# Two hybrid encoder layers on one core: score products over all 128 rows with stacked operands, units of q and k one step ahead, a gate back in the attention

## The chip, the cores and the metric

The kernel runs on 1 core of a Trainium2 chip. The metric is device time in microseconds: the median of the runs, beside one profiled execution, from whose trace all single durations are taken.

## The reference

Two layers over a sequence x of 512 tokens and 1024 channels. In each layer one input projection of x feeds three branches, whose outputs are gated, added and projected; then comes a layer norm. The change is in branch B, the differential attention:

```python
def _diff_attention(q, k, v, lam):           # 8 heads, 2 halves c of 64 channels each
    ...
    def block(qblk):
        s = jnp.einsum('bqhcd,bkhcd->bhcqk', qblk, k) * scale
        p = jax.nn.softmax(s.astype(jnp.float32), axis=-1)
        w = p[:, :, 0] - lam * p[:, :, 1]
        return jnp.einsum('bhqk,bkhe->bqhe', w, vf)
...
merged = (gates[:, :, 0] * (y_ssd @ w_br_ssd) + gates[:, :, 1] * (y_diff @ w_br_diff)
          + gates[:, :, 2] * (y_cross @ w_br_cross))      # gates = sigmoid(x @ w + b)
```

q and k go through a rotary embedding first. Branch A is a state-space scan (SSD) in both directions with 32 heads, branch C a cross attention into 256 memory tokens.

## The kernel before

Every large product is made in three passes: each operand is split into a high part (a copy by ACT, rounded to the matmul's format) and a low part (DVE: the value less its high part), and low times high, high times low and high times high add up in one bank of PSUM (`mm3`, line 103 for the matmul itself). Weights come in **units** of 128 x 1024 values: SP loads one (wr), ACT and DVE split it (wh, wl), and `proj` runs 24 products of 128 x 512 over it. `self.T` collects the whole program as a plan of units and steps; `emit` loads a unit two plan places ahead, into two buffers wr, and splits it into three buffers wh and wl.

The order on PE in the attention is written out by hand (`manual_schedule`). On DVE, ACT and SP the scheduler of the framework sets the order from its own costs when the kernel is built, and the engine then takes its instructions one after another in that order. Each DMA is issued by SP, which also stands still in its queue until what the next DMA waits for is there.

A layer runs its branches A, C and B one after the other and then the output projection. In branch A, four groups g of four blocks b: `zpart` is a unit, `ypart` builds for two heads the masked decay matrices (ab: a DMA, DVE, eight times ACT's exp, DVE) into m, and PE multiplies m with xsT (pm<-m,xsT). As PE has less work there than the others, gates of branches C and B that are needed later are computed in between: the table AHEAD names after which (g, b) which gate (branch, block) stands. A gate computed ahead is stored to memory (dgt<-tg) and loaded again in its branch.

In branch B, a head h has one unit each for q, k, v and the gate path g (two halves of a unit pair make the v of two heads). `rope` takes a unit's product out of PSUM (ACT, into rx), lets four DMAs write it with its 32-row quarters swapped (rsw), and adds rx times cos and rsw times sin on DVE. The result x has the first half c = 0 of the head's channels in rows 0 to 63 and the second in rows 64 to 127, and is split into q0 and q1, or k0 and k1 (high and low). `scores` works on a block of 128 queries (s = 4h + block): per half c three products over 64 rows, into a bank each; DVE takes the row minimum of each bank (fmx; q carries a factor of -1/8), ACT the exponential, and DVE the difference of the two maps (fpp). `turn` transposes fpp on PE and splits it (wT), `values` multiplies with v.

The attention is a list of steps s = 0 to 34, and each carries one unit: first the scores of s + 1, then half of the unit, then `values` and `turn` of s, then the other half. What a unit gives is needed by a later step, and its work on ACT, DVE and SP runs beside PE. For head h the units stand as rope(h + 1, q), rope(h + 1, k) and then two of g (h even) or two of v (h odd).

```python
units += [rope(h + 1, "q"), rope(h + 1, "k")]
units += [gpart(h), gpart(h + 1)] if h % 2 == 0 else [vpart(h + 1), vpart(h + 2)]
```

Seven of the eight gates of B follow as the last units (`gate(j)`); the eighth, block 0, is in AHEAD.

## Time and profile before

| | |
|---|---|
| median of 3 runs | 2222.38 us (2219.97 to 2222.85) |
| profiled execution, its own time | 2223.68 us |
| its span | 2221.9 us, granted clock of TensorE 0.997 |
| busy share of the span | PE 98%, DVE 71%, ACT 45%, POOL 2% |
| first attention, 715 to 985 us | PE busy 268.34 of 270 us |
| score products (pm<-k,q) | 384 of 64 x 128 by 64 x 512 |
| transfers | 283.73 MB, queue of SP 42.4% of 16 engines' span |

PE is TensorE's matmuls, PEld its weight loads, DVE VectorE, ACT ScalarE, POOL GpSimd, and SPq the queue in which SyncE issues DMAs. A row of the timeline has the start and the length in us, then engine, line, operation and the tiles; matmuls overlap in the records, so their spacing is read from start to start. A row of the waits has the time in all, how often, and the longest.

### The profile page before, as it was taken

Reading aid. Unit: us, or ns where it says so; the run is one execution under the profiler, and the core shown is the slowest. Engines: PE = TensorE matmul, PEld = TensorE weight load, DVE = VectorE, ACT = ScalarE, POOL = GpSimd, SP = SyncE. Lnnn points to the kernel's source line nnn. Section 1 sums busy time; section 2 is a strip of 40 time slices with the busy share of each in tenths; the row PEclk is TensorE's granted clock in tenths of the full one; section 3 lists DMA queues with packets and bytes.
Section 4 is the critical chain, followed back from the end, with each engine's and each line's share of the span. In section 5 each row is a group of like instructions: output and inputs, shape, how many; then the busy total and the mean of one; then the engine's idle time right before and its main releaser. Section 6 shows DMA issues by size and latency. Waiting matters only on the chain.

```text
span 2221.9 us, 29523 instructions
## 1 busy us (share of the span) xinstructions
PE 2171.0 (98%) x11330; PEld 1768.0 (80%) x11330; DVE 1585.9 (71%) x2440; ACT 1004.3 (45%) x1895; POOL 54.2 (2%) x38
## 2 busy tenths in 40 slices
PE   8999999999999999999999999999999999999998
PEld 6787877788887888878887777777788887888786
DVE  7887878758554777766467888888754547777567
ACT  5664545424442454543355564545423324554440
POOL 0000000000000000000000100000100000000000
PEclk9999999999999999999999999999999999999999
DMA  4654554425553322224564654454434333222353
GB/s 149 182 160 144 144 136 144 125 86 167 168 173 117 95 85 79 77 89 147 152 214 122 177 146 145 133 152 132 124 105 132 105 113 94 75 84 81 91 154 112
DMA packets 106162, 283.73 MB, mean 128 GB/s; under 512 B 12524, under 2 KB 13092, under 8 KB 105764
## 3 DMA queue, kind: packets, MB, share of 16 engines
q1 hardware_dynamic: 106020, 281.84, 42.4%
q8 instruction: 89, 1.46, 0.3%
q14 instruction: 53, 0.43, 0.1%
HBM read 255.55 MB, written 17.85 MB: 123 GB/s over the span
## 4 chain that ended last, share of the span: by engine, by line
PE 71%; DVE 14%; DMA 8%; ACT 5%; issue 1%; POOL 0%; SPq 0%; POOLq 0%; DVEq 0%; ACTq 0%
PE pj L103 55%; PE pm L103 13%; DMA ab<-dab 5%; DVE wl L81 3%; PE pt L111 2%; DVE ab L81 2%; DVE acc L84 2%; ACT ab L91 1%; ACT wh L91 1%; DMA wr<-wu 1%; DVE y L81 1%; DVE rx L81 1%; PE pt L103 1%; DMA fth<-rd 1%; DVE m L81 1%
## 5 line engine op out<-in xcount | busy, mean ns | idle before, releaser
L103 PE MATMUL pj<-xh,wl 128*128 128x512 f32 x1664 | 669.2, 402 | 11.0 <-DVE wl L81 8.9
L103 PE MATMUL pj<-xh,wh 128*128 128x512 f32 x1664 | 661.0, 397 | 0.0
L103 PE MATMUL pj<-xl,wh 128*128 128x512 f32 x1664 | 658.5, 396 | 0.0
L81 DVE TENSOR_TENSOR wl<-wr,wh 128x1024 fp32r<-128x1024 f32 x330 | 405.7, 1230 | 109.0 <-ACT wh L91 108.1
L91 ACT ACTIVATE wh<-wr 128x1024 fp32r<-128x1024 f32 x330 | 347.4, 1053 | 228.4 <-PE pj L103 147.4
L103 PEld LDWEIGHTS pj<-xh,wl 128*128 128x128 f32 x1664 | 313.9, 189 | 91.2 <-issue 18.3
L103 PEld LDWEIGHTS pj<-xh,wh 128*128 128x128 f32 x1664 | 313.8, 189 | 71.7 <-issue 5.7
L103 PEld LDWEIGHTS pj<-xl,wh 128*128 128x128 f32 x1664 | 314.2, 189 | 63.6 <-issue 3.6
L91 ACT ACTIVATE ab<-ab,bias 128x128 f32<-128x128 f32 x512 | 160.8, 391 | 120.5 <-DVE ab L81 119.7
L84 DVE SCALAR_TENSOR_TENSOR acc<-pj,hcw,acc 128x510 f32<-128x510 f32 x192 | 142.4, 744 | 24.2 <-ACT acc L91 22.8
L91 ACT ACTIVATE fpp<-pm,fmx 128x512 f32<-128x512 f32 x128 | 87.9, 687 | 84.3 <-DVE fmx L889 83.6
L889 DVE TENSOR_REDUCE fmx<-pm 128x1 f32<-128x512 f32 x128 | 87.0, 686 | 45.9 <-PE pm L103 45.5
L103 PE MATMUL pj<-yl,wh 128*128 128x512 f32 x256 | 102.4, 400 | 0.9 <-DVE yl L84 0.9
L103 PE MATMUL pj<-yh,wh 128*128 128x512 f32 x256 | 103.0, 403 | 0.0
L81 DVE TENSOR_TENSOR ab<-ab,cst 128x1024 f32<-128x1024 f32 x64 | 85.4, 1334 | 24.4 <-DMA ab<-dab 24.4
L103 PE MATMUL pj<-dy,wh 128*128 128x512 f32 (+1 forms) x384 | 102.2, 354 | 0.1
L103 PE MATMUL pj<-yh,wl 128*128 128x512 f32 x256 | 102.0, 399 | 0.0
L103 PE MATMUL pj<-cy,wh 128*128 128x512 f32 x256 | 78.8, 389 | 0.0
L103 PEld LDWEIGHTS pj<-dy,wh 128*128 128x128 f32 x384 | 67.8, 189 | 11.0 <-DVE dy L81 0.9
L103 PE MATMUL pj<-wh,xl 128*128 128x256 f32 x256 | 74.8, 292 | 0.0
L81 POOL TENSOR_TENSOR sqa<-sqa,sz 128x512 f32<-128x512 f32 x32 | 52.9, 1654 | 845.6 <-ACT sz L91 845.6
L103 PE MATMUL pj<-wl,xh 128*128 128x256 f32 x256 | 72.4, 283 | 0.0
(273 smaller groups left out, 3269.1 us busy)
## 6 DMA issues: line engine op xcount, KB each, us to landing
wr<-wu SPq DMA_DIRECT2D x336, 512.0 KB, 3.7
ab<-dab SPq DMA_DIRECT2D x64, 512.0 KB, 5.7
eb<-deb SPq DMA_DIRECT2D x64, 256.0 KB, 4.7
mkv<-dkv SPq DMA_DIRECT2D x16, 512.0 KB, 4.5
rsw<-rx SPq DMA_DIRECT2D x128, 64.0 KB, 2.0
dgt<-tg SPq DMA_DIRECT2D x18, 256.0 KB, 2.8
dkv<-mo SPq DMA_DIRECT2D x16, 256.0 KB, 4.2
dkv<-q SPq DMA_DIRECT2D x16, 256.0 KB, 3.6
```

Source lines behind the costliest of these rows:

```text
L81: (eng or self.nc.vector).tensor_tensor(out=out, in0=a, in1=b, op=op)
L84: self.nc.vector.scalar_tensor_tensor(out=out, in0=a, scalar=s, in1=b, op0=op0, op1=op1)
L91: self.nc.scalar.activation(out=out, in_=a, func=f, **kw)
L103: self.nc.tensor.matmul(out=out, lhsT=a, rhs=b, start=first, stop=last)
L111: self.nc.tensor.transpose(out=out, in_=x, identity=self.ident)
L889: nc.vector.tensor_reduce(out=mx[:, c:c + 1], in_=ps, axis=AX.X, op=ALU.min)
```

## The change

- **Stacked operands.** `rope` splits into one tile qkh with two planes, high and low, and four more DMAs stack them by half c. For k: k0 and k1 are now one tile for each half c, with the high part in rows 0 to 63 and the low part in rows 64 to 127. For q: a tile for each half and head, with both planes twice, in rows 0 to 63 and again in rows 64 to 127; it lies in the place that dy0 takes later (the tile of all q is called dy0).
- **Scores.** Per half c two products over 128 rows, ql and then qh against the stacked k, half 0 first, then half 1. (Low times low is added too.)
- **Order of units.** q of head 1 stands before the attention's steps. For head h come rope(h + 1, k), the two of g or v, then rope(h + 2, q): k a step earlier than before, q a whole head ahead of its use.
- **Gates.** Block 0 of B's gate is again a unit of the attention, without its way through memory. In the SSD's last group the one other gate stands behind b = 1 instead of b = 0.
- **Tiles.** dy is made only after the last scores; the residual of the output projection is loaded into fth, the next layer's memory rows into qkh.

```diff
-         (2, 0): [(2, 5)], (2, 2): [(2, 6)], (3, 0): [(2, 7)], (3, 2): [(1, 0)]}
+         (2, 0): [(2, 5)], (2, 2): [(2, 6)], (3, 1): [(2, 7)]}
...
-                self.qk[h, nm] = [self.t(fp, [P, S], f"{nm}{i}", F32R) for i in range(2)]
-                self.split(*self.qk[h, nm], x)
+                hl = self.t(fp, [P, 2, S], "qkh", F32R)
+                self.split(hl[:, 0, :], hl[:, 1, :], x)
+                half = [slice(64 * c, 64 * c + 64) for c in range(2)]
+                if nm == "q":
+                    o = [self.qst[:, 4 * (h % 2) + 2 * c:4 * (h % 2) + 2 * c + 2, :] for c in range(2)]
+                    self.qk[h, nm] = [[t[:, i, :] for i in range(2)] for t in o]
+                    parts = [(o[c][r], hl[half[c]]) for c in range(2) for r in half]
+                else:
+                    o = self.qk[h, nm] = [self.t(fp, [P, S], f"k{c}", F32R) for c in range(2)]
+                    parts = [(o[c][half[i], :], hl[half[c], i, :]) for c in range(2) for i in range(2)]
+                for to, src in parts:
+                    nc.sync.dma_start(out=to.bitcast(F32), in_=src.bitcast(F32))
...
-            for n, (a, b) in enumerate(((ql, kh), (qh, kl), (qh, kh))):
-                for c in range(2):
-                    rows = slice(64 * c, 64 * c + 64)
-                    self.mm(pss[c], a[rows, qs], b[rows, :], n == 0, n == 2)
+            for c in range(2):
+                (qh, ql), k = self.qk[h, "q"][c], self.qk[h, "k"][c]
+                self.mm(pss[c], ql[:, qs], k, True, False)
+                self.mm(pss[c], qh[:, qs], k, False, True)
...
+        step(rope(1, "q"), (), ())
...
-                units += [rope(h + 1, "q"), rope(h + 1, "k")]
+                units.append(rope(h + 1, "k"))
                 units += [gpart(h), gpart(h + 1)] if h % 2 == 0 else [vpart(h + 1), vpart(h + 2)]
+            if h + 2 < KC:
+                units.append(rope(h + 2, "q"))
```

What the built programs hold, at three places of the first layer's attention. All are about head 2, whose first scores are s = 8. A name ends in its tile's number.

PE, from the end of the unit ahead of the scores s = 8 (v of head 3, pj), before:

```order
L103 MATMUL pj_1146_6762<-wh_1106_6576,xh_5_82 128x256
L103 MATMUL pm_1157_6842<-k0_1135_6733,q1_1121_6658 128x512
L103 MATMUL pm_1158_6843<-k0_1135_6733,q1_1121_6658 128x512
L103 MATMUL pm_1157_6842<-k1_1136_6734,q0_1120_6657 128x512
L103 MATMUL pm_1158_6843<-k1_1136_6734,q0_1120_6657 128x512
L103 MATMUL pm_1157_6842<-k0_1135_6733,q0_1120_6657 128x512
L103 MATMUL pm_1158_6843<-k0_1135_6733,q0_1120_6657 128x512
L103 MATMUL pj_1145_6761<-wh_1123_6663,xl_6_83 128x256
```

and now:

```order
L103 MATMUL pj_1133_6711<-wh_1106_6594,xh_5_82 128x256
L103 MATMUL pm_1157_6880<-k0_1121_6676,dy0_1002_6016 128x512 x2
L103 MATMUL pm_1158_6881<-k1_1122_6677,dy0_1002_6016 128x512 x2
L103 MATMUL pj_1159_6893<-xh_5_82,wl_1125_6685 128x512
```

Six products over 64 rows became four over 128 rows, the two of one half c in turn, and both ask for the stacked k of their half (k0, k1); the unit that follows is q of head 3.

DVE, from the softmax of s = 7 to the low part of head 2's k, before (rx_1133 is its rotary tile):

```order
L893 RECIPROCAL fsm_1141_6744<-fsm_1141_6744 128x1
L88 TENSOR_SCALAR fsm_1141_6744<-fsm_1141_6744,fs0_1015_6065,nlam_1012_6059 128x1
L81 TENSOR_TENSOR rx_1133_6723<-rx_1133_6723,cos_750_4281 128x512
L81 TENSOR_TENSOR rsw_1134_6725<-rsw_1134_6725,sin_751_4282 128x512
L84 SCALAR_TENSOR_TENSOR fpp_1142_6745<-fpp_1142_6745,fsm_1141_6744 128x512
L81 TENSOR_TENSOR rx_1133_6723<-rx_1133_6723,rsw_1134_6725 128x512
L81 TENSOR_TENSOR wT1_1149_6801<-pt_1150_6802,wT0_1148_6800 128x4x128
L81 TENSOR_TENSOR k1_1136_6734<-rx_1133_6723,k0_1135_6733 128x512
```

and now (rx_1118 is the rotary tile, qkh_1120 the split, v0 and v1 the split of a unit of v):

```order
L903 RECIPROCAL fsm_1139_6774<-fsm_1139_6774 128x1
L88 TENSOR_SCALAR fsm_1139_6774<-fsm_1139_6774,fs0_1008_6029,nlam_1005_6023 128x1
L81 TENSOR_TENSOR v1_1148_6860<-pj_1132_6710,v0_1147_6859 128x256
L84 SCALAR_TENSOR_TENSOR fpp_1140_6775<-fpp_1140_6775,fsm_1139_6774 128x512
L81 TENSOR_TENSOR rx_1118_6663<-rx_1118_6663,cos_744_4246 128x512
L81 TENSOR_TENSOR rsw_1119_6665<-rsw_1119_6665,sin_745_4247 128x512
L81 TENSOR_TENSOR wT1_1145_6827<-pt_1146_6828,wT0_1144_6826 128x4x128
L81 TENSOR_TENSOR rx_1118_6663<-rx_1118_6663,rsw_1119_6665 128x512
L81 TENSOR_TENSOR v1_1150_6862<-pj_1132_6710,v0_1149_6861 128x256
L81 TENSOR_TENSOR qkh_1120_6673<-rx_1118_6663,qkh_1120_6673 128x512
```

Before, k's unit belongs to step s = 5 and now to s = 4; its products on DVE stand in both behind the same softmax of s = 7, in the step just ahead of their use, now behind fpp instead of around it, and the wT product of the turn moved ahead of the sum.

SP, from the load of a weight unit ahead of the swap of head 2's k, before:

```order
L138 DMA wr_1137_6737<-wu 128x1024
L828 DMA rsw_1119_6649<-rx_1118_6647 32x512 x4
L138 DMA wr_1151_6833<-wu 128x1024
L828 DMA rsw_1134_6725<-rx_1133_6723 32x512 x4
L138 DMA wr_1164_6924<-wu 128x1024
```

and now (rsw_1119 is the swap of k, qkh_1104 the split of head 2's q, qkh_1120 that of its k):

```order
L138 DMA wr_1135_6767<-wu 128x1024
L829 DMA rsw_1119_6665<-rx_1118_6663 32x512 x2
L846 DMA dy0_1002_6016<-qkh_1104_6585 64x1024 x4
L829 DMA rsw_1119_6665<-rx_1118_6663 32x512 x2
L138 DMA wr_1151_6871<-wu 128x1024
L138 DMA wr_1164_6942<-wu 128x1024
L846 DMA k0_1121_6676<-qkh_1120_6673 64x512 x2
L846 DMA k1_1122_6677<-qkh_1120_6673 64x512 x2
L138 DMA wr_1182_7032<-wu 128x1024
```

The stacks of q (four transfers into dy0) now stand between the first two and the last two quarters of k's swap; behind two loads of weights come the four quarters of k's stack, and behind these the next load.

## The prediction

> **What bounds the kernel now.** I read the page first for the busiest engine, then the waits of PE for what it is ever short of, then the timeline of one attention step on each engine, because the change lives there.

> ```profile
> PE 2171.0 (98%) x11330; PEld 1768.0 (80%) x11330; DVE 1585.9 (71%) x2440; ACT 1004.3 (45%) x1895; POOL 54.2 (2%) x38
> PE 71%; DVE 14%; DMA 8%; ACT 5%; issue 1%; POOL 0%; SPq 0%; POOLq 0%; DVEq 0%; ACTq 0%
> ```

> PE is busy 98% of the span and carries most of the chain that ended last. So a matmul less is time less, as long as its operands are there; and a wait of PE is time lost in full, since nothing else fills it (in the attention PE follows an order written by hand).

> ```profile
> PE pm L103 <- DVE m L81: 8.2, 8, 2.3
> PE pm L103 <- DVE k L81: 2.3, 11, 0.2
> PE pm L103 <- ACT k L91: 0.4, 2, 0.2
> ```

> These are the waits that the change touches: those of the SSD's products for m, and those of the score products (pm<-k,q) for k. The second kind is small but tells most: in 16 heads PE waits 13 times for k, up to 0.2 us each. Its margin is already nothing. One such head, on PE, DVE, ACT and SP:

> ```profile
> 785.46 0.39 PE L103 MATMUL pj<-xh,wh 128*128 128x512 f32 x1
> 785.78 0.96 PE L103 MATMUL pm<-k,q 64*128 64x512 f32 x6
> 794.47 0.50 PE L103 MATMUL pm<-k,q 64*128 64x512 f32 x2
> 795.13 0.73 PE L103 MATMUL pm<-k,q 64*128 64x512 f32 x4 [0.16 <-DVE k L81]
> 795.78 0.39 PE L103 MATMUL pj<-wh,xl 128*128 128x256 f32 x1
> ...
> 791.13 0.68 DVE L81 TENSOR_TENSOR rx<-rx,cos 128x512 f32<-128x512 f32 x1
> 791.73 0.69 DVE L81 TENSOR_TENSOR rsw<-rsw,sin 128x512 f32<-128x512 f32 x1
> 792.99 0.69 DVE L81 TENSOR_TENSOR rx<-rx,rsw 128x512 f32<-128x512 f32 x1
> 794.38 0.69 DVE L81 TENSOR_TENSOR k<-rx,k 128x512 fp32r<-128x512 f32 x1
> 799.79 0.74 DVE L84 SCALAR_TENSOR_TENSOR fpp<-fpp,fsm 128x512 f32<-128x512 f32 x1
> ...
> 793.71 0.64 ACT L91 ACTIVATE k<-rx 128x512 fp32r<-128x512 f32 x1 [1.42 <-DVE rx L81]
> ...
> 786.51 2.41 SPq L828 DMA_DIRECT2D rsw<-rx  x4
> ```

> The unit of k ends near 785.7 (785.46 and one slot of 0.23). One step later, at 794.47, the next head's scores begin with the high half of k; the low half ends on DVE at 795.07, and PE waits 0.16. What fixes 795.07 is DVE's order, not the swap through DMA, which was issued by 788.9: the rotary products stand behind the softmax of the step.

> **The change, part by part.**

> *Six half-row score products become four of full rows.* The cost of a group is read where it stands between full-size products:

> ```profile
> 818.28 0.39 PE L103 MATMUL pj<-xh,wh 128*128 128x512 f32 x1
> 818.60 0.96 PE L103 MATMUL pm<-k,q 64*128 64x512 f32 x6
> 819.49 0.50 PE L103 MATMUL pj<-xh,wl 128*128 128x512 f32 x1
> 819.83 0.39 PE L103 MATMUL pj<-xl,wh 128*128 128x512 f32 x1
> 820.06 0.40 PE L103 MATMUL pj<-xh,wh 128*128 128x512 f32 x1
> ```

> A full-size product takes a slot of 0.23 us (819.83 to 820.06). From 818.28 to 819.83 are 1.55 us; less two slots, of the products at 818.28 and 819.49, the group costs 1.09. Six products in 1.09 are less than six slots (1.38), so the two halves of the rows do run side by side: three slots (0.69) and some 0.4 for going into the half-row form and out again. Four full products cost 4 x 0.23 = 0.92. Saved: 0.17 a group, times 64 groups (32 a layer) = 11 us. DVE and ACT do what they did; the weight loads, four for six, lie beside PE.

> [...]

> *The waits for k of before* (2.3 + 0.4) are in the old time and are replaced by what follows: -2.7.

> *The stacking transfers.* Each unit of q or k now writes its high and low halves into one tile (qkh), and four more DMAs on SP put them on top of each other. For k they stand between DVE's last product and PE. k's unit is one step earlier, but the order built for DVE keeps its rotary products where they were against their use: behind the softmax (fpp) of the last step before it, and now behind a wT product too. So the step gained goes into waiting. Let U be the end of the unit before that step.
> - The softmax ends 4.75 after the scores (800.53 against 795.78). The scores take 0.92: U + 5.67.
> - Then the cos and sin products and wT at 0.60 from start to start, the sum (0.69): U + 8.16. ACT's copy (0.64) to U + 8.85. DVE's difference (0.69) to U + 9.6; before it was 795.07 - 785.69 = 9.38.
> - SP issues k0's high half from U + 8.85, its low half from 9.6, k1's two behind it.

> ```profile
> L828 SPq DMA_DIRECT2D rsw<-rx x128: 507/588/598, 721.8 to 2056.4; - x128
> DMA to landing us min/median/max: 1.9/2.0/3.3
> L655 SPq DMA_DIRECT2D dgt<-tg x18: 326/330/459, 80.2 to 1583.9; - x18
> ```

>   No transfer of this size within SBUF is in the trace. The nearest is the swap (rsw), 64 KB: 0.6 an issue, 2.0 to landing. The nearest lower issue is the gate's store, 0.33. With the swap's numbers k1's last quarter is issued at U + 10.8 and lands at U + 12.8.
> - The second pair of products would start 0.46 into the scores. The step, 8.78 before (785.69 to 794.47), is 8.6 long without those 0.17 with a unit of v, about 8.3 with one of g (24 slots of 0.23 for v's 5.76). So PE stands 12.8 - 9.06 = 3.7 or 12.8 - 8.76 = 4.0; g's own sdy product puts DVE 0.1 later: 4.1. Mean 3.9.

> Of the seven later heads a layer, six have this form: 12 x 3.9 = 47. Head 1 has its products ahead of the softmax's end (two products less, 1.3) and both high halves issued first (0.6): 2.0, two times, 4. Together 51. Ends: with 0.33 an issue, 1.9 to landing and DVE done at 9.4, 12 x 2.9 + 2 = 37; with a landing of 3.3, 12 x 5.2 + 2 x 3.3 = 69. I take the swap's values, as it is the same kind of transfer.

> *Head 0.* k's first use was without slack too:

> ```profile
> L103 PE MATMUL pm<-k,q x384: 383/394/502, 735.1 to 2087.2; 64*128 64x512 f32 x192
> L81 DVE TENSOR_TENSOR k<-rx,k x16: 684/693/693, 734.6 to 2062.7; 128x512 fp32r<-128x512 f32 x16
> ```

> The difference ended at 735.3, the scores began at 735.1. Now q of head 1 stands between (24 slots, 5.5 us), which covers 1.2 + 2.0 for the last quarter. 0, at most 1 a layer.

> *q, one head ahead.* Its four transfers (256 KB each) stand on SP ahead of two quarters of k's swap, which so lands some 8.5 us after k's unit; DVE wants it at about 8 + 5.7. Hidden, by 5 us. The weight loads (wr) queued behind k's quarters belong to splits that DVE reaches two steps later. Both 0; the cover is gone if a stack were held up by a further step.

> *The gate of B for block 0 goes from the SSD's last group into the attention* (24 slots, 5.5 us a layer, the same work), and the gate behind b = 0 goes behind b = 1. Its store and load go, both hidden: 0. It counts only where PE then waits in the SSD:

> ```profile
> 420.19 1.09 PE L103 MATMUL pm<-m,xsT 128*64 128x128 f32 x16
> 433.67 1.09 PE L103 MATMUL pm<-m,xsT 128*64 128x128 f32 x16
> 445.78 1.09 PE L103 MATMUL pm<-m,xsT 128*64 128x128 f32 x16
> ...
> 413.38 0.69 DVE L84 SCALAR_TENSOR_TENSOR sz<-th,pj 128x512 f32<-128x512 f32 x1 [3.68 <-ACT th L91]
> 431.27 0.69 DVE L81 TENSOR_TENSOR m<-ab,gs 128x512 f32<-128x512 f32 x1
> 443.86 0.69 DVE L81 TENSOR_TENSOR m<-ab,gs 128x512 f32<-128x512 f32 x1
> ```

> m is ready at 431.96 and 444.55, 1.7 and 1.2 ahead of PE; PE would now come 5.5 earlier. But DVE stood still for 3.68 us at 413 behind that earlier gate, and can run ahead too. Between -1 (a shorter wait) and 5.5 a layer; I take 1, near the lower end, since the idle 3.68 and the margin of 1.2 nearly make up the 5.5: +2 in all.

> The late tiles (dy made after the last scores, the residual's in fth) are needed more than a step after they come free: 0.

> **Sum:** -11 - 2.7 + 51 + 2 = +39. The profiled run took 2223.68 (span 2221.9), 1.3 above the median of 2222.38; from the median that is 2261 us.

> **Rivals.**
> - *k is in time* (the other side). If DVE had k by U + 5.9 (9.06 less 1.2 and 2.0), the wait would be nothing: -11 - 2.7 + 2 = -12, 2211. For it: the unit is a whole step earlier. Against it: DVE takes its instructions in the order shown, and the products stand behind a softmax that ends at 5.67. It decides at 3.7 us.
> - *The stalls cool PE's clock.* The trace has one long idle of PE, at the start:

> ```profile
> 6.89 0.77 PE L103 MATMUL pj<-xh,wl 128*128 128x512 f32 x1 [6.89 <-DVE wl L81]
> 8.42 0.63 PE L103 MATMUL pj<-xh,wl 128*128 128x512 f32 x1
> 8.85 0.63 PE L103 MATMUL pj<-xl,wh 128*128 128x512 f32 x1
> 10.82 0.40 PE L103 MATMUL pj<-xh,wl 128*128 128x512 f32 x1
> ```

>   Products come at 0.43 instead of 0.23 until 10.6: 8 x 0.2 = 1.6 lost. Behind 12 stalls that is 19: 2280. Against it: the stall is broken in two, about 3.2 (k0) and 0.7 (k1), half of that first idle. [...]
> - *The SSD loses the whole gate* in both layers: +11 for +2, 2270.

> **Chances.** Late k as summed (with the SSD's share between its ends): 0.80. In time: 0.10. Clock: 0.07. The rest, other queues held up: 0.03. The bounds of the first case are 37 - 13.7 - 2 = +21 and 69 - 13.7 + 11 = +66, so 2243 to 2288, which takes in the clock's 2280; I go down to 2240, which leaves out the case in time. A change under 0.2% (4.4 us) can't be told from none here. Faster 0.10, same 0.02, slower 0.88.

> **What would show it.** Right: the waits of PE name k<-qkh as a DMA, 14 times at 2 to 5 us, about 50 us in all, with k0's wait longer than k1's; score products of 128 rows, 256 of them, at 0.23 from start to start and no gap around them; DVE's softmax row just ahead of the cos product of k. In the SSD, waits for m within a few us of 8.2. Wrong: waits for k of under 1 us (then the quarters land sooner than the swap does, or DVE is done earlier), a granted clock under 0.95 in the attention, or waits for wl there, which would mean that the stacks hold up the weights.

## The result, and the profile after

The changed kernel takes 2290.69 us (median of 4 runs, 2287.45 to 2291.75), the kernel before 2221.18 beside it: a ratio of 1.0315, 95% interval 1.0303 to 1.0328, or 70 us more (67 to 73). The forecast was 2261, and its range ended at 2288. The profiled execution took 2290.76 us (span 2289.0, granted clock 0.984; before 0.997).

The page's busy shares and chain, in the form shown of before:

```profile
PE 2190.3 (96%) x11202; PEld 1805.0 (79%) x11202; DVE 1588.3 (69%) x2440; ACT 1001.8 (44%) x1895; POOL 53.6 (2%) x38
PE 71%; DVE 14%; DMA 8%; ACT 4%; issue 2%; SPq 1%; POOL 0%; POOLq 0%; DVEq 0%; ACTq 0%
```

PE has 128 matmuls fewer and is busy 19 us longer, in a span that is 67 us longer. So there are two things to find: time in which PE stands still, and matmuls that take longer. The waits of PE (us in all, how often, the longest), those that answer to the rows of before:

```profile
PE pm L103 <- DMA k<-qkh: 51.3, 24, 4.9
PE pm L103 <- DVE m L81: 7.6, 8, 1.4
PE pj L103 <- DVE wl L81: 3.7, 3, 2.4
PE pm L103 <- DMA rsw<-rx: 1.0, 2, 0.5
```

The waits for k by DVE and ACT are gone, and 51.3 us for the stacked k by DMA stand there, at the first scores of heads 1 to 7 in both layers (24 rows: at ten of these 14 places PE waits twice, for half 0 and for half 1). The wait for wl stood at 10.1 before, 6.9 of it at the start of the kernel, which is now put down to xh. Next the two attentions as stretches, from the first scores to the norms; the columns are us, busy time of PE, PEld, DVE, ACT and POOL with the number of instructions, then the granted clock. First the kernel before, then the changed one:

```profile
735.13:989.58 254.45, 251.37 (x1454) 202.59 (x1454) 186.50 (x328) 128.36 (x258) 0.00 (x0) 1.00 0.29 84
1839.51:2093.87 254.36, 251.25 (x1453) 202.54 (x1452) 186.53 (x328) 128.39 (x258) 0.00 (x0) 1.00 0.30 84
```

```profile
735.84:1022.22 286.38, 258.82 (x1388) 220.04 (x1388) 187.40 (x327) 126.78 (x258) 0.00 (x0) 0.95 0.43 112
1873.12:2158.92 285.80, 258.68 (x1388) 219.89 (x1388) 187.24 (x327) 126.79 (x257) 0.00 (x0) 0.95 0.43 112
```

They are 31.9 and 31.4 us longer, 63.4 of the 67.1 by which the spans differ. The clock is 0.95 in both, against 1.00. One place on PE shows both losses, the step into head 2 that the prediction had worked out:

```profile
798.29 0.28 PE L103 MATMUL pj<-wh,xh 128*128 128x256 f32 x1
801.55 0.71 PE L103 MATMUL pm<-k,dy 128*128 128x512 f32 x2 [2.98 <-DMA k<-qkh]
802.88 1.08 PE L103 MATMUL pm<-k,dy 128*128 128x512 f32 x2 [0.62 <-DMA k<-qkh]
803.76 0.63 PE L103 MATMUL pj<-xh,wl 128*128 128x512 f32 x1
804.18 0.63 PE L103 MATMUL pj<-xl,wh 128*128 128x512 f32 x1
804.61 0.63 PE L103 MATMUL pj<-xh,wh 128*128 128x512 f32 x1
...
806.32 0.44 PE L103 MATMUL pj<-xh,wl 128*128 128x512 f32 x1
```

PE waits 2.98 for half 0 of k and 0.62 for half 1. Then products of 128 x 512 come every 0.43 us instead of 0.23, up to 806.4. The windows cut at these points show the granted clock:

```profile
799.59:803.00 3.41, 0.83 (x3) 0.45 (x4) 2.25 (x3) 0.62 (x2) 0.00 (x0) 1.00 0.93 190
803.00:806.41 3.41, 3.41 (x9) 2.65 (x10) 1.50 (x4) 1.56 (x4) 0.00 (x0) 0.50 0.31 122
837.13:840.54 3.41, 0.94 (x3) 0.56 (x4) 2.03 (x3) 0.22 (x1) 0.00 (x0) 1.00 0.91 186
840.54:843.96 3.41, 3.41 (x9) 2.64 (x9) 1.71 (x4) 1.55 (x4) 0.00 (x0) 0.50 0.30 121
```

For exactly 3.41 us PE runs at half clock and is busy all the time: 1.7 us lost. This stands behind 14 of the 14 waits: 12 x 1.7, and at the last head of each layer a slow stretch of 6.8 us, of which 4.0 lie behind the end of the wait, 2 x 2.0. That makes 24.5 us. Outside the attentions this trace has four slow stretches past its start, against two before; 2 x 1.7 = 3.4 us are most of the other 3.7 by which the spans differ.

### The profile page after: what moved, and what is told of

The parts are those of the page before. It is cut to its first block, busy times and chain, and to the rows that moved or that the text cites. A ratio compares the mean times of both kernels' runs of the same rounds, so it can differ in the third digit from the quotient of the medians.

```text
span 2289.0 us, 29601 instructions
## 1 busy us (share of the span) xinstructions
PE 2190.3 (96%) x11202; PEld 1805.0 (79%) x11202; DVE 1588.3 (69%) x2440; ACT 1001.8 (44%) x1895; POOL 53.6 (2%) x38
## 4 chain that ended last, share of the span: by engine, by line
PE 71%; DVE 14%; DMA 8%; ACT 4%; issue 2%; SPq 1%; POOL 0%; POOLq 0%; DVEq 0%; ACTq 0%
PE pj L103 55%; PE pm L103 13%; DMA ab<-dab 3%; DVE wl L81 2%; PE pt L111 2%; DVE ab L81 2%; DMA k<-qkh 1%; DVE acc L84 1%; DVE y L81 1%; SPq L846 1%; ACT wh L91 1%; ACT ab L91 1%; DMA fth<-rd 1%; DMA wr<-wu 1%; DVE m L81 1%
## 5 line engine op out<-in xcount | busy, mean ns | idle before, releaser
L103 PE MATMUL pj<-xh,wl 128*128 128x512 f32 x1664 | 672.5, 404 | 11.8 <-ACT xh L91 7.1
L103 PE MATMUL pj<-xh,wh 128*128 128x512 f32 x1664 | 667.9, 401 | 0.0
L103 PE MATMUL pj<-xl,wh 128*128 128x512 f32 x1664 | 666.6, 401 | 0.0
L81 DVE TENSOR_TENSOR wl<-wr,wh 128x1024 fp32r<-128x1024 f32 x330 | 404.4, 1226 | 116.9 <-ACT wh L91 116.3
L91 ACT ACTIVATE wh<-wr 128x1024 fp32r<-128x1024 f32 x330 | 347.4, 1053 | 244.9 <-PE pj L103 165.5
L103 PEld LDWEIGHTS pj<-xh,wl 128*128 128x128 f32 x1664 | 319.3, 192 | 82.9 <-ACT xh L91 7.0
L103 PEld LDWEIGHTS pj<-xh,wh 128*128 128x128 f32 x1664 | 318.5, 191 | 72.9 <-issue 5.7
L103 PEld LDWEIGHTS pj<-xl,wh 128*128 128x128 f32 x1664 | 319.1, 192 | 67.8 <-issue 3.6
L91 ACT ACTIVATE ab<-ab,bias 128x128 f32<-128x128 f32 x512 | 160.5, 391 | 110.5 <-DVE ab L81 108.9
L84 DVE SCALAR_TENSOR_TENSOR acc<-pj,hcw,acc 128x510 f32<-128x510 f32 x192 | 142.2, 743 | 24.5 <-ACT acc L91 23.3
L103 PE MATMUL pm<-k,dy 128*128 128x512 f32 x256 | 79.3, 425 | 52.7 <-DMA k<-qkh 51.3
L91 ACT ACTIVATE fpp<-pm,fmx 128x512 f32<-128x512 f32 x128 | 87.4, 685 | 73.3 <-DVE fmx L899 71.5
L103 PE MATMUL pj<-dy,wh 128*128 128x512 f32 (+1 forms) x384 | 103.4, 358 | 0.3 <-DVE dy L81 0.2
L103 PE MATMUL pj<-yl,wh 128*128 128x512 f32 x256 | 102.6, 401 | 0.9 <-DVE yl L84 0.9
L103 PE MATMUL pj<-yh,wh 128*128 128x512 f32 x256 | 103.1, 403 | 0.0
L103 PEld LDWEIGHTS pm<-k,dy 128*128 128x128 f32 x256 | 46.8, 195 | 70.9 <-DMA k<-qkh 42.1
L103 PE MATMUL pj<-yh,wl 128*128 128x512 f32 x256 | 102.3, 400 | 0.0
L81 DVE TENSOR_TENSOR ab<-ab,cst 128x1024 f32<-128x1024 f32 x64 | 84.7, 1323 | 20.5 <-DMA ab<-dab 20.3
L81 DVE TENSOR_TENSOR wT<-pt,wT 128x512 fp32r<-128x512 f32 x64 | 44.0, 688 | 52.3 <-ACT wT L91 52.3
L103 PE MATMUL pj<-cy,wh 128*128 128x512 f32 x256 | 78.7, 389 | 0.0
L91 ACT ACTIVATE wT<-pt 128x512 fp32r<-128x512 f32 x64 | 38.2, 597 | 92.2 <-PE pt L111 92.1
```

What stands on the lines that cost most here:

```text
L81: (eng or self.nc.vector).tensor_tensor(out=out, in0=a, in1=b, op=op)
L84: self.nc.vector.scalar_tensor_tensor(out=out, in0=a, scalar=s, in1=b, op0=op0, op1=op1)
L91: self.nc.scalar.activation(out=out, in_=a, func=f, **kw)
L103: self.nc.tensor.matmul(out=out, lhsT=a, rhs=b, start=first, stop=last)
```

## The experiments

The first theory was: the stacked k is late (51 us), and each late k also slows the clock (25 us). The rivals were that the traffic or the issues of the stacking cost the time, and that the 25 us come from elsewhere. Differences below are the ratio, with its interval, times 2220 us.

**k two steps ahead.** Only the units' order of the changed kernel is altered:

```diff
-        units = []
-        for h in range(KC):
-            if h + 1 < KC:
-                units.append(rope(h + 1, "k"))
-                ...
+        units = [rope(1, "k"), gpart(0)]
+        for h in range(2, KC):
+            units += [rope(h, "k"), rope(h, "q")]
+            units += {2: [gpart(1), gpart(2)], 3: [vpart(2), vpart(3)], ...}[h]
```

> The changed kernel with the units of the attention in another order: k of head h + 1 is the first unit of head h - 1's second step instead of head h's first, so it stands two steps ahead of its scores; all transfers, products and splits are the same. Theory (k is late by 51 us of waits, and each of the 14 waits leaves PE at half clock for some 1.8 us, 25 us more): both vanish, waits of PE for k under 3 us in all, no products at 0.43 in the attention, and what is left is the shorter scores and the old waits for k: 2221 - 11 - 2.7 = 2208, between 2203 and 2213. Rival (the 64 + 64 stacking transfers cost time by their traffic or by their place on SP, whenever they are issued): the waits of PE move to other tiles (wl, m, q's stack), and the time stays above 2235.

Measured: 2219.00, ratio 0.9996 (0.9986 to 1.0006). All but two of the waits for k went, with the slow products behind them, and the rival is out. But the time is 11 us above what the theory gave. A part of the 11 is plainly seen: head 1 in both layers, whose unit stands where it stood.

```profile
762.54 1.36 PE L103 MATMUL pm<-k,dy 128*128 128x512 f32 x4 [1.97 <-DMA k<-qkh]
1866.61 2.05 PE L103 MATMUL pm<-k,dy 128*128 128x512 f32 x4 [2.14 <-DMA k<-qkh]
```

These waits are 4.1 us. Behind each stands one slow stretch of 3.41 us, with PE busy in it for 3.41 and 3.34 (in the second it holds the four score products too), so 3.4 us more. The remaining 3.5 are the question of the kernels with the order and the gate, below.

**The stack is issued but not read.** The changed kernel, with scores from the split itself:

```diff
-                    o = self.qk[h, nm] = [self.t(fp, [P, S], f"k{c}", F32R) for c in range(2)]
+                    o = [self.t(fp, [P, S], f"k{i}", F32R) for i in range(2)]
+                    self.split(*o, x)
+                    self.qk[h, nm] = o
...
-                    parts = [(o[c][half[i], :], hl[half[c], i, :]) for c in range(2) for i in range(2)]
+                    parts = [(hl[half[i], c, :], o[i][half[c]]) for c in range(2) for i in range(2)]
```

> The changed kernel, but the scores read the split of k itself (the high plane for half 0, the low plane for half 1) instead of its stack; the four stacking transfers of each k are issued as before, from the same split, into tiles that nothing reads. So the products are the same in number and size, with other numbers in them, and the score's value is not the reference's. Theory (PE waits for the landing of the stack): k is there with DVE's difference at U + 9.6 or ACT's copy at U + 8.85, against scores that start at U + 8.3 to 8.6 and take 0.46 a half: waits of 0.3 to 0.7 at 14 places, some 7 us in all, no cooling: 2221 - 11 + 5 = 2215, between 2207 and 2220. Rival (the traffic and the issues on SP are what costs): 2280 to 2291 as in the changed kernel.

Measured: 2223.22, ratio 1.0010 (1.0000 to 1.0020). With all 64 + 64 transfers in their places, 68 of the 70 us are gone: it is the waiting for the stack, not its traffic. PE waits for k at 8 places, six of 0.4 us and two of 1.3, where 14 of 0.3 to 0.7 and 7 us in all were expected:

```profile
PE pm L103 <- ACT k L91: 4.8, 8, 1.3
```

The time is 3 us above the expected range, though the profiled execution (2216.88, the lowest of its ten runs) is inside it. The granted clocks of the ten runs show where the rest is: the two runs at 0.998 took 2216.88 and 2217.77, the eight at 0.995 and 0.996 took 2221.7 to 2225.92, and 0.002 to 0.003 of 2220 are 4 to 7 us of slow clock. Which waits brought the slow stretches can't be seen, as only one run has a trace.

**The four products alone**, in the kernel before:

```diff
-            for n, (a, b) in enumerate(((ql, kh), (qh, kl), (qh, kh))):
-                for c in range(2):
-                    rows = slice(64 * c, 64 * c + 64)
-                    self.mm(pss[c], a[rows, qs], b[rows, :], n == 0, n == 2)
+            for c in range(2):
+                self.mm(pss[c], ql[:, qs], (kh, kl)[c], True, False)
+                self.mm(pss[c], qh[:, qs], (kh, kl)[c], False, True)
```

> The kernel before with only the form of the score products changed: two products over 128 rows for each half, against the split of k itself (high plane for half 0, low plane for half 1), no stacking, the units in the order of before; the score's value is not the reference's. Theory (a group costs 0.92 instead of 1.09): 64 x 0.17 = 11 us less, 2210, between 2207 and 2214, with waits for k as before or up to 3 us more, since half 1 is now reached 0.46 after the scores began. Rival (going into the half-row form and out again costs nothing that lasts, since what follows hides it): 2217 to 2225.

Measured: 2209.85, ratio 0.9954 (0.9942 to 0.9966): -10 us (-13 to -8) against -11. In the changed kernel a group without a wait shows the size directly; from its start to the next product are 0.93 us, four slots and no gap:

```profile
810.96 1.10 PE L103 MATMUL pm<-k,dy 128*128 128x512 f32 x4
811.89 0.39 PE L103 MATMUL pj<-xh,wl 128*128 128x512 f32 x1
```

**The order and the gates alone**: the kernel before with the changed order of units, the changed table of gates and the late tiles, half-row products and split tiles as before.

> The kernel before with the changed order of units and the changed gates alone: six score products over half the rows as before, from the split tiles, no stacking. It asks what the order costs by itself, since the kernel with k two steps ahead is 9 us above the one with the four products alone. Theory (of these 9, some 2.5 are the SSD's waits behind the gate that left, the rest are waits for stacks of heads 0 and 1 with what follows them): without stacks -2.7 for the waits for k and +2.5 in the SSD, 2220, between 2216 and 2223. Rival (the order itself is worth the 9, by other waits): 2226 to 2230.

Measured: 2220.85, ratio 1.0010 (0.9999 to 1.0021): +2 us (0 to 5). The theory's 2220 holds, the rival's 9 is out. No wait for k is left, and with the same number of products both attentions are 3.9 to 4.0 us shorter than before:

```profile
732.51:982.98 250.47, 249.06 (x1454) 202.59 (x1453) 184.50 (x324) 126.98 (x257) 0.00 (x0) 1.00 0.28 82
1836.13:2086.61 250.48, 249.06 (x1454) 202.62 (x1454) 184.54 (x324) 126.98 (x257) 0.00 (x0) 1.00 0.28 82
```

So the waits for k of before cost some 8 us, not the 2.7 of their rows. Most of it is in the first group of each head, where PE waits between the products: from its start to the next product it takes 1.30 us before and 0.89 here, on the mean of 16. As the whole is +2 all the same, order, gates and late tiles cost some 10 outside the attentions. By the granted clocks, 0.9960 on the mean of these 12 runs and 0.9975 of the 18 of the kernel before beside them, 0.0015 x 2220 = 3.3 us of it are further slow stretches. The traces, one execution each, don't show where the rest lies. Now the kernel with k two steps ahead adds up: -10, +2 and 7.5 for head 1 are -0.5; measured were -0.9 (-3 to 1).

**The gate alone**, in the kernel before: the table of gates as changed, the gate of block 0 behind the units.

```diff
-         (2, 0): [(2, 5)], (2, 2): [(2, 6)], (3, 0): [(2, 7)], (3, 2): [(1, 0)]}
+         (2, 0): [(2, 5)], (2, 2): [(2, 6)], (3, 1): [(2, 7)]}
```

> The kernel before with its gates alone changed: block 0 of B's gate a unit of the attention again, the other gate of the SSD's last group behind b = 1. The prediction had +2 for it (-2 to 11). By the rows of the kernels with k two steps ahead and with the unread stack, PE waits 1.1 to 1.65 us for m in that group, once a layer: +2.5, 2222.5, waits for m in the last group of each SSD. Rival (DVE runs ahead as far as PE does): no wait there, 2220.

Measured: 2236.48, ratio 1.0077 (1.0061 to 1.0093): +17 us, far above either. But the edit was not the one meant. Without q of head 1 ahead of the steps, the list of units is one longer than the steps that need them, so a gate stands behind the attention's tail, and PE waits there for the norms; this row is from the end of layer 1:

```profile
2124.74 1.52 PE L103 MATMUL pm<-cst,rs_y 128*128 128x128 f32 x6 [3.03 <-DVE rs_y L81]
```

From stage to stage in the traces, the tails are 3 and 4 us longer than before (beside the gate's own 5.5) and the second attention 5, and the SSD has waits for m of 8.6 in all against 8.2. The waits for k rose too, from 2.7 to 7.8. The mean granted clock is 0.9943 against 0.9975, so some 7 of the 17 us are slow stretches. So the kernel says little of the SSD; the +17 belongs to an edit with the longer list in it, and is not divided further.

**Filling the wait.** If it is the idle time that slows the clock, work that is of no use to anyone helps. In the changed kernel 13 products, or 6, or 9, stand ahead of the first scores of each head but the first:

```diff
+            if qc == 0 and h:
+                d = self.bank(self.pm, "pm")
+                for i in range(13):
+                    self.mm(d, self.xh[:, 0, :P], self.xh[:, 1, :], i == 0, i == 12)
```

> The changed kernel with 13 products more (128 x 128 by 128 x 512, into a bank of PSUM that nothing reads) in front of the first scores of each head but the first: 13 x 0.23 = 3.0 us of work where PE stood still for k, 14 times. Theory (behind each wait the products come at 0.43 instead of 0.23 for some 1.8 us a stall): k still lands when it did, so the filled steps end no later, but no clock is lost: the waits for k fall from 51 to some 15 us, the products stay at 0.23, and the time is 2291 - 25 = 2266, between 2260 and 2276. Rival (the idle time does not slow PE; the 25 us beyond the waits come from elsewhere, as loads that came late): the fill changes nothing, 2288 to 2296.

Measured: 2272.31, ratio 1.0241 (1.0226 to 1.0256). 182 matmuls more make the kernel 16 us faster, the rival's "nothing" is out. A slow stretch stands behind 1 of the 14 places instead of 14, and apart from it the attentions run at full clock:

```profile
736.93:1012.37 275.44, 267.98 (x1480) 228.56 (x1481) 186.85 (x327) 126.25 (x257) 0.00 (x0) 1.00 0.44 116
1860.51:2138.40 277.89, 269.61 (x1482) 229.64 (x1481) 187.10 (x327) 126.86 (x258) 0.00 (x0) 0.99 0.44 116
```

Together they are 18.9 us shorter than in the changed kernel. The 24.5 are not reached, since one slow stretch is left (1.7) and the fill with what is left of the waits (42.0 + 12.6) is 3.3 longer than the 51.3 that it fills: 24.5 - 1.7 - 3.3 = 19.5.

> As the filled kernel, with 6 products in front of the first scores of each head instead of 13: 1.4 us, so PE stands still for some 1.6 us at 6 of the 14 places, 2.1 at 6, 3.4 at 2. Theory (an idle time slows PE only from about 2 us on): no slow products at the 6 shorter ones, some at the others; 2291 - 6 x 1.8 = 2280, down to 2272 if the 2.1 do not slow it either. Rival (every idle time over 1 us slows it): slow products behind 14 of 14, 2288 to 2292.

Measured: 2288.52, ratio 1.0313 (1.0294 to 1.0332): the rival's time. Behind 12 of the 14 places the clock still falls, though the waits are down to 33.6 us and at six of these places are 1.6 + 0.6 us. One of them, in windows cut where the slow stretch begins:

```profile
798.56:801.98 3.41, 1.68 (x7) 0.75 (x5) 2.18 (x5) 1.23 (x3) 0.00 (x0) 1.00 0.78 169
801.98:805.39 3.41, 2.95 (x7) 2.40 (x8) 1.44 (x3) 1.56 (x4) 0.00 (x0) 0.50 0.43 143
```

My threshold of 2 us fell. But "every wait over 1 us" could not be the rule either: in the same trace PE waits 2.07 us for wl, and the next products come every 0.23. So I put down when each slow stretch of a trace begins. In the changed kernel 802.998, 840.545 and 878.091 are 37.55 us apart, 11 x 3.4133; 448.012 and 526.518 are 23 x 3.4133. All slow stretches of that trace lie on one grid of 3.4133 us, and the heads do not move it: the first scores of heads 2 to 6 follow each other 37.33 to 37.51 us apart, the slow stretches behind them 37.55 each time. (The heads are close to 11 periods apart, so their waits fall nearly alike on the grid, and 14 of 14 or 6 of 6 are not as many independent trials.) In the last rows PE was busy 1.68 of 3.41 us and lost the next stretch. In the changed kernel's attentions the busiest stretch that was followed by a slow one had 1.48, and the idlest of the whole kernel, past its start, that was not had 1.54. Here are a pair of the first kind and that one:

```profile
949.77:953.18 3.41, 1.36 (x5) 0.89 (x6) 2.13 (x3) 0.51 (x2) 0.00 (x0) 1.00 0.89 214
953.18:956.60 3.41, 3.41 (x10) 2.64 (x9) 1.88 (x4) 1.17 (x4) 0.00 (x0) 0.50 0.16 65
...
1250.14:1253.55 3.41, 1.54 (x7) 0.93 (x5) 1.76 (x3) 1.40 (x4) 0.00 (x0) 1.00 1.05 209
1253.55:1256.97 3.42, 3.30 (x9) 1.72 (x10) 3.40 (x7) 3.41 (x9) 0.00 (x0) 1.00 1.09 205
```

This makes a theory with a number: half of a stretch. The fill of 9 was run to test it.

> As the filled kernels, with 9 products in front of the first scores of each head: 2.1 us, so of the two waits 0.9 + 0.6 us are left at 6 of the 14 places, 1.4 + 0.6 at 6, 2.8 at the two of the last head. Theory (the clock is set for stretches of 3.413 us on a grid that runs on by itself; a stretch is at half clock if PE was busy for less than about half of the one before, 1.7 us): 1.5 us idle never slows, 2.0 only where the grid falls so that over 1.7 of it lies in one stretch, 2.8 mostly; so slow stretches behind 2 to 6 of the 14 places, all starting at whole multiples of 3.413 us from each other, and a time of 2272 + 3 to 8, 2274 to 2281. Rival (any wait of over 1 us slows PE): slow behind 8 of 14, 2282 to 2286.

Measured: 2267.75, ratio 1.0228 (1.0203 to 1.0252): as fast as with 13 products (the intervals overlap), and below what the theory gave. One slow stretch is left behind the 14 places, against 2 to 6 and 8. The rival is out: waits of 1.4 + 0.6 at four places (not six) and of 2.8 at two slowed PE once. Of the four, three lay across two stretches, with PE busy for 2.0 and 2.8 us in them; the fourth fell into one, with PE busy for 1.46, and that is the one that slowed it. Of the wait of 2.84 at the last head, 1.04 lie in one stretch and 1.80 in the one before it, which had PE busy for 1.61, just under half; the next stretch was granted in full:

```profile
971.87:975.28 3.41, 1.61 (x8) 0.99 (x6) 2.52 (x3) 1.73 (x3) 0.00 (x0) 1.00 0.37 86
975.28:978.70 3.41, 2.38 (x10) 1.79 (x11) 1.30 (x2) 0.85 (x3) 0.00 (x0) 1.00 0.83 221
```

The three slow stretches left in this trace outside its two ends begin at 1173.259, 1623.819 and 1961.738, 132 and 99 times 3.4133 apart. So the grid holds, and the limit is near half, but not sharp: 1.61 was enough here, 1.68 was not with the fill of 6.

**A version that beats both.** With k two steps ahead, k of head 1 also goes ahead of the steps:

```diff
         step(rope(1, "q"), (), ())
-        step(vpart(0), (), ())
-        step(vpart(1), (), (job(scores, 0),))
-        units = [rope(1, "k"), gpart(0)]
+        step(rope(1, "k"), (), ())
+        step(vpart(0), (), (job(scores, 0),))
+        units = [vpart(1), gpart(0)]
```

> The kernel with k two steps ahead, and beside it k of head 1 as a unit ahead of the attention's steps (behind q of head 1), with the second half-unit of v, v1, in its place as the first unit of the steps; so head 1, whose k is a unit of head 0's first step there, has it in time too. Theory: the two waits for k of 2.0 and 2.1 us and the slow products behind them (1.5 and 0.6 by their spacing) go, nothing else changes: 2219 - 6 = 2213, between 2210 and 2216. Rival (the place ahead is as crowded: k of head 0 comes later by its queue on SP, or v1 is late for its values): the waits turn up at the first scores or at the values, 2218 to 2222.

Measured: 2210.79, ratio 0.9962 (0.9948 to 0.9975): -8 us (-12 to -6), at the lower end of what was expected, as head 1 was worth 7.5 and not 6. No wait for k on its stack is left, and both attentions take 246.5 us at full clock, 8 less than before:

```profile
736.23:982.72 246.49, 244.90 (x1412) 213.74 (x1413) 186.54 (x327) 123.98 (x257) 0.00 (x0) 1.00 0.49 130
1836.85:2083.40 246.55, 244.90 (x1413) 213.73 (x1413) 186.45 (x327) 124.41 (x257) 0.00 (x0) 1.00 0.50 130
```

That is 16 in the attentions and 8 in the whole: the other stages are longer. In the traced run, the slowest of its seven, five slow stretches lie outside the attentions past the start, against two before, which is 5 us of it.

## Why the prediction was right and wrong

- **Four products for six, -11.** Right: -10 (-13 to -8) alone, 0.93 a group.
- **The waits for k of before, -2.7.** They are gone, but the term was too small: the attentions of the order alone say some 8. The total hides it, since order, gates and late tiles cost more elsewhere.
- **Late k, +51.** Right, 51.3, and by its steps. That it meets to the last us is partly luck: the ten heads in the middle wait 3.75 on the mean and the last head of each layer 4.85, where 3.9 was forecast for all twelve. With U = 789.87, SP issues the first quarter at 798.46 (U + 8.6, forecast 8.85), and the second pair of products starts at 802.88 (U + 13.0, forecast 12.8). DVE's order is the one that was read: softmax, cos, sin, wT, sum, difference. A quarter of the stack, 128 KB, behaves nearly as the swap's 64 KB do: 0.63 from issue to issue (2.51 for four) against 0.60, 2.3 from issue to landing against 2.0. These are rows of DVE, then of SP in that step, then of the page's DMA issues:

```profile
794.62 0.74 DVE L84 SCALAR_TENSOR_TENSOR fpp<-fpp,fsm 128x512 f32<-128x512 f32 x1
795.28 0.68 DVE L81 TENSOR_TENSOR rx<-rx,cos 128x512 f32<-128x512 f32 x1
...
798.47 0.69 DVE L81 TENSOR_TENSOR qkh<-rx,qkh 128x512 fp32r<-128x512 f32 x1 [0.36 <-ACT qkh L91]
```

```profile
798.46 2.51 SPq L846 DMA_DIRECT2D k<-qkh  x4
```

```profile
k<-qkh SPq DMA_DIRECT2D x64, 128.0 KB, 2.3
```

- **Head 0, 0 or at most 1 a layer.** 0.9 in layer 0 and 0.5 in layer 1, at that bound.
- **q a head ahead, 0.** Right: no wait of PE names q's stack.
- **The gate out of the SSD, +2.** Waits for m fell to 7.6 in all, though one of 1.2 stands in the last group. Order, gates, late tiles and the waits for k that are gone make +2 together where -0.7 was summed, 3 us more. How much of that is the gate's stays open, as the kernel with the gate alone had another edit in it.
- **The clock, rival at 0.07.** This is the step that failed. The prediction made late k and the slow clock two cases to choose from, and set the second aside with "the stall is broken in two, about 3.2 (k0) and 0.7 (k1), half of that first idle". But the second is a consequence of the first, not another case. The size was near (1.6 a stall forecast, 24.5 / 14 = 1.75 measured), in part by luck: 1.6 was read off the kernel's start, where products come every 0.43 us up to 10.6 in the trace of before, 11.1 in that of the changed kernel and 12.7 in that with the fill of 9, each time to where that trace's grid falls. It belonged into the sum: 39 + 24.5 are 63.5, with 1.4 for head 0 and those 3 us for the order 68, against 70 measured (67 to 73). The fill shows that idle time is the cause: with PE kept busy through the same stalls by 13 products the slow stretches go behind 13 of the 14 places.

The trace of before had the counterexample to that argument, and I had not read it. PE waits 1.21 us for sqa and then runs eight products of one column:

```profile
453.29 1.05 PE L103 MATMUL pt<-cst,sqa 128*128 128x1 f32 x8 [1.21 <-POOL sqa L81]
454.20 0.65 PE L103 MATMUL pj<-xl,wh 128*128 128x512 f32 x1
454.64 0.63 PE L103 MATMUL pj<-xh,wh 128*128 128x512 f32 x1
```

```profile
450.94:454.35 3.41, 2.21 (x15) 1.67 (x14) 1.18 (x2) 0.39 (x1) 1.77 (x1) 1.00 0.51 143
454.35:457.76 3.41, 3.41 (x9) 2.64 (x10) 2.00 (x13) 0.00 (x0) 0.00 (x0) 0.50 0.03 11
```

A wait of 1.2 us with little work behind it cost a whole slow stretch, so a single idle time of 6.89 was no scale for what a stall needs. Why this stretch, with 2.21 us busy by the records, counted as idle, no run tests. In the kernel with the fill of 6 two waits of 1.6 + 0.6 us were enough 6 times of 6, though at nearly the same place of the grid.

## What to carry to other kernels

Here a stall of PE had two prices: its length, and 1.7 us more (2.0 at the last head of each layer) where it left PE busy for less than 1.5 of a 3.41 us stretch of the grid. By this limit it is an estimated 2 x (3.41 - 1.5) = 3.8 us of wait from which on no place on the grid can save it. Before a step is moved earlier, look at what the engine behind it will have queued in front of its work; here "one step earlier" was taken back by the softmax on DVE (its row at 794.62 stands ahead of k's cos product at 795.28), and two steps earlier, with k of head 1 ahead of the steps too, turned +70 us into -8. And when a rival follows from the forecast's own cause, add it to the sum instead of giving it a chance of its own.
